# Placing the halves of every weight tile 64 and 192 bytes, modulo 256, from the rows that stream through TensorE

## The chip, the cores and the metric

The kernel runs on one core of a Trainium2 chip. The metric is the device time of one execution in microseconds (us), lower is better; the times given are medians over executions.

## The reference

A trunk of four decoder layers works on `x` of 256 tokens by 1024 features in float32. Each layer is a feed-forward block (SwiGLU, hidden size 2816), a token mixer (latent attention, differential attention, a Mamba-2 scan, then latent attention again) and a second feed-forward block. Each of the twelve sub-layers is

```
y = fn(x * (1 + scale) + shift)
x = layernorm(alpha * x + weight * gate * y)
```

where shift, scale and gate come from `silu(c) @ w_mod + b_mod`. Almost all of the arithmetic lies in the products of 256 token rows with weight matrices:

```
gate, up = split(h @ w_in, 2)          # 1024 x 5632
y = (silu(gate) * up) @ w_out          # 2816 x 1024
```

About 500 MB of float32 weights are read once, and every product has to keep float32 accuracy.

## The kernel before, in words

**Three products for one.** TensorE multiplies in the type `F32R`, which holds fewer bits than float32. So each operand is split into a high half (the value as the type holds it) and a low half (what is missing), and `mm3` (line 485) issues three matmuls for each product: high weights with high rows, high weights with low rows, low weights with high rows.

```
T.matmul(out=ps, lhsT=wh, rhs=xh, start=first, stop=False)
T.matmul(out=ps, lhsT=wh, rhs=xl, start=False, stop=False)
T.matmul(out=ps, lhsT=wl, rhs=xh, start=False, stop=last)
```

The weights (`lhsT`, 128 columns, 512 bytes of each SBUF partition) are loaded into the array, and the activations (`rhs`, 256 columns, 1024 bytes of each partition) stream through. The weights of a matmul are loaded again for each of the three, and the load of the next matmul's weights lies beside the streaming of the present one.

**Where the operands lie.** All of SBUF is laid out once, by the calls of `pool` in `trunk` (lines 442 to 453). The rows that stream are in `hwh` and `hwl` (high and low halves of the modulated input) or in tiles of `g` (hidden activations). Every tile between `g` and the weight ring has a size that is a multiple of 256 bytes (`g` 2048, `wraw` 4096, `hwh` and `hwl` 9216, and so on), so all rows that stream in the full products start at the same address modulo 256. The split weights are in the ring `wr` of 16 tiles of 4096 bytes, and behind the ring come the small tiles: constants, masks, statistics. With `WSTEP = 16`, `Slots.__init__` (line 117) puts an unused gap of 16 floats (64 bytes) behind every second tile of the ring. So tiles `wr0` and `wr1` lie 0 bytes, modulo 256, from the rows, `wr2` and `wr3` 64, `wr4` and `wr5` 128, `wr6` and `wr7` 192, `wr8` and `wr9` 0 again, and so on: both halves of a weight have one offset, and the four offsets take turns.

**How the ring is filled.** `take` (line 593) fetches the next weights in half items of four 128-row blocks by 256 columns: SP issues one DMA of 512 KB into `wraw`, ScalarE copies it into the tile of the high half, and VectorE subtracts and writes the low half (`split`, line 507). One half item serves 4 x 2 x 3 = 24 matmuls. Ring tiles are handed out by `Program.place` (line 207) in the order in which they came free; after some sub-layers the pairs come out with the high half in the odd tile.

**What sets the order.** A planner in the program (`Program.schedule`) orders all instructions from fixed costs that know nothing of addresses; each engine then runs its list in order, and semaphores hold it where data are late. Between the half items, `gm_mac` streams the modulation weights `w_mod` through `wraw` and accumulates them on VectorE, by the quotas in `PLAN`.

At the start of each sub-layer `pre_mms` (line 874) multiplies the rows before their normalization is known. There the rows are 258 columns wide, and `hwh` steps by 288 floats (1152 bytes) from one block of 128 to the next, so odd blocks lie 128 bytes off.

Of the kernel before, what the change touches and what calls it, by code (L numbers as in the profile page):

```python
# [10 lines left out]
F32 = mybir.dt.float32  # L11
F32R = mybir.dt.float32r
# [43 lines left out]
class Ref:  # L56


    def __init__(self, root, fns):
        self.root, self.fns, self.ap = root, fns, None  # L60
# [52 lines left out]
class Slots:  # L113

    def __init__(self, pool, name, n, elems, psum=False, dt=F32, fresh=False, step=0):
        self.pool, self.name, self.elems, self.psum, self.dt, self.fresh = pool, name, elems, psum, dt, fresh
        self.tiles = []
        for i in range(n):  # L120
            self.tiles.append(self.make(i, dt))
            if step and i % 2:
                pool.tile([128, step], F32, name=f"{name}gap{i}", tag=f"{name}gap{i}")
        self.free = list(range(n))
        self.hist, self.old, self.owner = [[] for _ in range(n)], [[] for _ in range(n)], [None] * n

# [292 lines left out]

WHOLE = (4, 7, 10)  # L420

WSTEP = 16

DEFER = {0: 3, 1: 3}

# [2 lines left out]
def trunk(ctx: ExitStack, tc: tile.TileContext, consts, x, c, positions, w_mod, b_mod, ln_g, ln_b,  # L428
# [8 lines left out]
    sb = ctx.enter_context(tc.tile_pool(name="sb", bufs=1))  # L437
    pp = ctx.enter_context(tc.tile_pool(name="pp", bufs=1, space=PSUM))
    PW, HP = S + 2, 288
    slots = {}  # L440

    def pool(name, n, elems, dt=F32, step=0):
        slots[name] = Slots(sb, name, n, elems, dt=dt, fresh=name == "g", step=step)

    slots["mm"] = slots["aux"] = Slots(pp, "mm", 8, 512, True)
    for name, n, elems in (("g", 25, 512), ("wraw", 8, 1024), ("gacc", 1, 3072), ("res", 1, 2048),
                           ("t256", 14, 256), ("sd", 1, 512), ("re", 1, 512)):
        pool(name, n, elems)
    for name, n, elems in (("hwh", 1, KD * HP), ("hwl", 1, KD * HP)):
        pool(name, n, elems, F32R)  # L450
    pool("wr", 16, 1024, F32R, WSTEP)
    for name, n, elems in (("dtr", 1, 128), ("w0", 1, 32), ("modc", 6, 24)):
        pool(name, n, elems)

# [308 lines left out]
    class Tail:  # L763
        def __init__(self, s, res, weight):
            self.s, self.d = s, res
            self.weight, self.w = weight, None
# [878 lines left out]
```

## Time and profile before

| what | value |
|---|---|
| median of three executions | 2103.96 us (2102.66 to 2103.96) |
| the profiled execution's own time | 2103.96 us |
| its span in the profile | 2102.2 us |
| granted TensorE clock, mean over the span | 0.998 |
| PE (matmuls) busy | 2074.9 us, 99% |
| DVE (VectorE), ACT (ScalarE) busy | 1713.0 us (81%), 1190.2 us (57%) |
| HBM traffic | 500.73 MB read, 239 GB/s over the span |

The profile names engines PE (matmuls of TensorE), PEld (its weight loads), DVE, ACT, POOL and SP. PE's busy time comes from matmuls whose ends are modelled, and consecutive matmuls overlap: one lasts some 280 ns, but the next starts after some 117 ns. So the pace of PE is read from starts and counts, not from the duration of one. A granted clock of 1.00 is 2.4 GHz.

### The profile page before, as it was taken

How to read it: one execution, taken by the hardware profiler on the slowest of the kernel's cores; microseconds unless marked ns; L12 is line 12 of the kernel's file. 1: busy time of each engine (PE TensorE's matmuls, PEld its weight loads, DVE VectorE, ACT ScalarE, POOL GpSimd, SP SyncE). 2: the span in 40 equal slices, each digit the busy share in tenths (PEclk: the TensorE clock that was granted, in tenths of full speed). 3: DMA queues.
4: the chain of work that ended last, by engine and by line, in shares of the span. 5: the costliest groups of instructions: out<-in, count | busy, mean ns of one | idle time of the engine just before them, and what ended most of it. 6: DMA issues, size and time to landing. Idle time of an engine off the chain costs nothing. (4 is left out here: it accounts for less than half of the span.)

```text
span 2102.2 us, 42927 instructions
## 1 busy us (share of the span) xinstructions
PE 2074.9 (99%) x17287; PEld 2011.6 (96%) x17287; DVE 1713.0 (81%) x2745; ACT 1190.2 (57%) x1836; POOL 98.5 (5%) x112
## 2 busy tenths in 40 slices
PE   8999999999999999999999999999999999999998
PEld 6999999999999999999999988899999999999998
DVE  4888899887887879977988798879887988879744
ACT  3554687536544786644654475547545644577543
POOL 0000100000000101000000011000000000100000
PEclk9999999999999999999999999999999999999999
DMA  9899657995989435997698654356986889545861
GB/s 312 281 346 326 206 188 249 342 304 187 319 309 324 149 103 161 350 326 256 191 354 304 206 159 140 112 157 197 355 281 205 302 305 323 163 130 186 261 186 45
DMA packets 410227, 504.58 MB, mean 240 GB/s; under 512 B 21937, under 2 KB 371244, under 8 KB 410028
## 3 DMA queue, kind: packets, MB, share of 16 engines
q1 hardware_dynamic: 410028, 501.84, 72.5%
q8 instruction: 135, 2.21, 0.4%
q14 instruction: 64, 0.52, 0.1%
HBM read 500.73 MB, written 1.05 MB: 239 GB/s over the span
## 5 line engine op out<-in xcount | busy, mean ns | idle before, releaser
L400 PE MATMUL mm<-hwh,wr 128*128 128x256 f32 (+1 forms) x6736 | 1222.2, 283 | 3.7 <-ACT hwh L400 1.9
L400 PEld LDWEIGHTS mm<-hwh,wr 128*128 128x128 f32 x6736 | 1041.1, 189 | 19.9 <-issue 14.1
L400 ACT ACTIVATE wr<-wraw 128x1024 fp32r<-128x1024 f32 (+3 forms) x705 | 700.7, 1003 | 577.2 <-PE mm L400 242.9
L400 PE MATMUL mm<-hwl,wr 128*128 128x256 f32 (+1 forms) x3368 | 955.7, 284 | 4.9 <-DVE hwl L400 4.8
L400 DVE TENSOR_TENSOR wr<-wraw,wr 128x1024 fp32r<-128x1024 f32 (+3 forms) x691 | 793.7, 1165 | 172.4 <-ACT wr L400 169.1
L400 PE MATMUL mm<-g,wr 128*128 128x256 f32 x5496 | 665.2, 282 | 1.4 <-DVE g L400 0.9
L400 PEld LDWEIGHTS mm<-g,wr 128*128 128x128 f32 x5496 | 652.9, 189 | 12.3 <-issue 8.3
L400 PEld LDWEIGHTS mm<-hwl,wr 128*128 128x128 f32 x3368 | 637.4, 189 | 11.1 <-DVE hwl L400 6.8
L400 DVE SCALAR_TENSOR_TENSOR gacc<-wraw,condc,gacc 128x1024 f32<-128x1024 f32 x238 | 307.2, 1291 | 7.9 <-DMA wraw<-in_w_mod_dram 7.2
L400 ACT ACTIVATE g<-mm 128x512 f32<-128x512 f32 (+4 forms) x208 | 105.7, 521 | 100.3 <-PE mm L400 98.7
L400 ACT ACTIVATE g<-g 128x512 fp32r<-128x512 f32 (+1 forms) x104 | 63.3, 625 | 36.0 <-DVE g L400 35.6
L400 PE MATMUL mm<-g,g 128*128 128x128 f32 (+2 forms) x464 | 81.6, 312 | 0.0
L400 DVE TENSOR_TENSOR g<-g,g 128x512 fp32r<-128x512 f32 (+2 forms) x111 | 75.4, 699 | 4.2 <-ACT g L400 3.4
L400 DVE TENSOR_TENSOR res<-res,re 128x256 f32<-128x256 f32 x171 | 68.0, 418 | 8.2 <-ACT re L400 7.9
L400 DVE TENSOR_TENSOR g<-g,mm 128x512 f32<-128x512 f32 x81 | 54.9, 680 | 19.6 <-PE mm L400 16.9
L400 PEld LDWEIGHTS mm<-g,g 128*128 128x128 f32 (+1 forms) x464 | 57.9, 175 | 7.4 <-ACT g L400 0.5
L400 ACT ACTIVATE t<-res 128x256 f32<-128x256 f32 x84 | 34.8, 416 | 48.1 <-DVE res L400 47.9
L400 POOL TENSOR_TENSOR res<-res,t 128x256 f32<-128x256 f32 x28 | 25.4, 932 | 708.9 <-ACT t L400 624.9
L400 DVE TENSOR_TENSOR res<-res,t 128x256 f32<-128x256 f32 x56 | 31.7, 581 | 23.9 <-ACT t L400 23.9
L400 DVE SCALAR_TENSOR_TENSOR res<-mm,gw,res 128x256 f32<-128x256 f32 x84 | 39.2, 475 | 14.2 <-PE mm L400 14.2
L400 ACT ACTIVATE t<-res,abcol 128x256 f32<-128x256 f32 x72 | 43.2, 601 | 9.3 <-DVE res L400 8.0
L400 ACT ACTIVATE res<-res,abcol 128x256 f32<-128x256 f32 x88 | 48.0, 588 | 0.0
(198 smaller groups left out, 1158.5 us busy)
## 6 DMA issues: line engine op xcount, KB each, us to landing
wraw<-in_ffn_w_in_dram SPq DMA_DIRECT2D x340, 512.0 KB, 6.1
wraw<-in_w_mod_dram SPq DMA_DIRECT2D x272, 512.0 KB, 6.8
wraw<-in_ffn_w_out_dram SPq DMA_DIRECT2D x128, 512.0 KB, 5.7
wraw<-in_ffn_w_out_dram SPq DMA_DIRECT2D x64, 384.0 KB, 5.7
wraw<-in_ssm_w_in_dram SPq DMA_DIRECT2D x32, 512.0 KB, 4.3
wraw<-in_diff_w_in_dram SPq DMA_DIRECT2D x24, 512.0 KB, 4.3
wraw<-in_w_mod_dram SPq DMA_DIRECT2D x32, 256.0 KB, 6.2
wraw<-in_mla_w_out_dram SPq DMA_DIRECT2D x16, 512.0 KB, 4.6
```

Of the source, the lines that this page charges most:

```text
L400: getattr(eng.real, method)(*[real(a) for a in args], **{k: real(v) for k, v in one.items()})
```

## The change

`Slots.__init__` takes a list of gaps in place of a step, and puts gap number i ahead of tile number i. For `wr` the list is 16 floats and then 15 times 32 floats, that is 64 bytes ahead of `wr0` and 128 bytes ahead of every later tile.

```diff
-    def __init__(self, pool, name, n, elems, psum=False, dt=F32, fresh=False, step=0):
+    def __init__(self, pool, name, n, elems, psum=False, dt=F32, fresh=False, gaps=()):
...
         for i in range(n):
+            if gaps and gaps[i]:
+                pool.tile([128, gaps[i]], F32, name=f"{name}gap{i}", tag=f"{name}gap{i}")
             self.tiles.append(self.make(i, dt))
-            if step and i % 2:
-                pool.tile([128, step], F32, name=f"{name}gap{i}", tag=f"{name}gap{i}")
...
-WSTEP = 16
+WGAPS = [16] + [32] * 15
...
-    pool("wr", 16, 1024, F32R, WSTEP)
+    pool("wr", 16, 1024, F32R, WGAPS)
```

All even tiles of the ring now lie 64 bytes, modulo 256, from the rows that stream, and all odd tiles 192. The ring takes 1472 bytes more of each partition, and the small tiles behind it move by that. Which tile a half item gets, and the order of instructions on every engine, stay as they were; the names in the built order differ in their running number alone.

This is a place in the engine order of PE where two half items are worked off in turns of six matmuls (start of a feed-forward block); a name such as `wr7_132` is ring tile 7 with the running number of its allocation. Before:

```order
L400 MATMUL mm1_62<-hwh0_120,wr7_132 128x256
L400 MATMUL mm1_62<-hwl0_121,wr7_132 128x256
L400 MATMUL mm1_62<-hwh0_120,wr6_131 128x256
L400 MATMUL mm1_62<-hwh0_120,wr7_132 128x256
L400 MATMUL mm1_62<-hwl0_121,wr7_132 128x256
L400 MATMUL mm1_62<-hwh0_120,wr6_131 128x256
L400 MATMUL mm7_68<-hwh0_120,wr11_138 128x256
L400 MATMUL mm7_68<-hwl0_121,wr11_138 128x256
L400 MATMUL mm7_68<-hwh0_120,wr10_137 128x256
```

And now:

```order
L400 MATMUL mm1_62<-hwh0_120,wr7_137 128x256
L400 MATMUL mm1_62<-hwl0_121,wr7_137 128x256
L400 MATMUL mm1_62<-hwh0_120,wr6_135 128x256
L400 MATMUL mm1_62<-hwh0_120,wr7_137 128x256
L400 MATMUL mm1_62<-hwl0_121,wr7_137 128x256
L400 MATMUL mm1_62<-hwh0_120,wr6_135 128x256
L400 MATMUL mm7_68<-hwh0_120,wr11_145 128x256
L400 MATMUL mm7_68<-hwl0_121,wr11_145 128x256
L400 MATMUL mm7_68<-hwh0_120,wr10_143 128x256
```

Nothing moved. The tile that is used twice holds the high half; here that is the odd one. Before, `wr7` and `wr6` lay at 192 and `wr11` and `wr10` at 64, so the offset changed every six matmuls; now the odd tiles lie at 192 and the even ones at 64, so it changes twice in every three.

The second place is a run of half items later on PE, before; the first row of each is shown:

```order
L400 MATMUL mm6_67<-hwh0_120,wr0_122 128x256
...
L400 MATMUL mm1_62<-hwh0_120,wr12_140 128x256
...
L400 MATMUL mm1_62<-hwh0_120,wr14_143 128x256
...
L400 MATMUL mm7_68<-hwh0_120,wr2_125 128x256
...
L400 MATMUL mm7_68<-hwh0_120,wr9_135 128x256
...
L400 MATMUL mm2_63<-hwh0_120,wr5_129 128x256
...
L400 MATMUL mm2_63<-hwh0_120,wr11_138 128x256
...
L400 MATMUL mm3_64<-hwh0_120,wr7_132 128x256
```

By the layout before, these eight half items lie at offsets 0, 128, 192, 64, 0, 128, 64 and 192. After the change each of them has one half at 64 and one at 192.

## Rows read from the trace of the kernel before

**Rows 1.** The page: span, busy time of the engines, and the granted clock in 40 slices.

```profile
span 2102.2 us, 42927 instructions
...
PE 2074.9 (99%) x17287; PEld 2011.6 (96%) x17287; DVE 1713.0 (81%) x2745; ACT 1190.2 (57%) x1836; POOL 98.5 (5%) x112
...
PEclk9999999999999999999999999999999999999999
```

**Rows 2.** Waits of PE, the longest kind: us in total, times, longest.

```profile
PE mm L400 <- DVE hwl L400: 4.8, 7, 1.6
```

**Rows 3.** Groups of PE by form: count, busy us, mean ns, idle before.

```profile
L400 PE MATMUL mm<-hwh,wr 128*128 128x256 f32 x5984 | 1082.5, 283 | 3.7 <-ACT hwh L400 1.9 <-ACT g L400 1.0 <-DVE wr L400 0.5
L400 PE MATMUL mm<-hwl,wr 128*128 128x256 f32 x2992 | 847.3, 283 | 1.8 <-DVE hwl L400 1.8
L400 PE MATMUL mm<-g,wr 128*128 128x256 f32 x5496 | 665.2, 282 | 1.4 <-DVE g L400 0.9 <-ACT g L400 0.2
L400 PE MATMUL mm<-hwh,wr 128*128 128x258 f32 x752 | 141.0, 285 | 0.0
L400 PE MATMUL mm<-hwl,wr 128*128 128x258 f32 x376 | 108.4, 288 | 3.1 <-DVE hwl L400 3.1
```

**Rows 4.** Windows, PE instructions on ring tiles alone: busy us (count), PEclk, DMA, GB/s.

```profile
360.00:480.00 120.00, 118.58 (x1012) 1.00 0.94 322
840.00:960.00 120.00, 119.50 (x1009) 1.00 0.92 317
1040.00:1160.00 120.00, 118.64 (x1022) 1.00 0.96 332
1640.00:1760.00 120.00, 118.64 (x1006) 1.00 0.93 321
```

**Rows 5.** Timeline of PE, second run of half items: start us, us, instruction.

```profile
1459.21 0.40 PE L400 MATMUL mm<-hwh,wr 128*128 128x256 f32 x2
...
1462.08 0.40 PE L400 MATMUL mm<-hwh,wr 128*128 128x256 f32 x2
...
1464.92 0.40 PE L400 MATMUL mm<-hwh,wr 128*128 128x256 f32 x2
...
1467.75 0.39 PE L400 MATMUL mm<-hwh,wr 128*128 128x256 f32 x2
...
1470.47 0.40 PE L400 MATMUL mm<-hwh,wr 128*128 128x256 f32 x2
...
1473.35 0.40 PE L400 MATMUL mm<-hwh,wr 128*128 128x256 f32 x2
...
1476.19 0.40 PE L400 MATMUL mm<-hwh,wr 128*128 128x256 f32 x2
...
1479.02 0.40 PE L400 MATMUL mm<-hwh,wr 128*128 128x256 f32 x2
...
1481.85 0.40 PE L400 MATMUL mm<-hwh,wr 128*128 128x256 f32 x2
```

**Rows 6.** Timeline of PE, the place with turns of six matmuls.

```profile
1029.32 0.40 PE L400 MATMUL mm<-hwh,wr 128*128 128x256 f32 x2
...
1034.77 0.39 PE L400 MATMUL mm<-hwh,wr 128*128 128x256 f32 x2
```

**Rows 7.** Timeline of PE in a stretch with 258 columns.

```profile
1017.85 0.41 PE L400 MATMUL mm<-hwh,wr 128*128 128x258 f32 x2
...
1023.60 0.40 PE L400 MATMUL mm<-hwh,wr 128*128 128x258 f32 x2
```

**Rows 8.** Windows, all: PE, PEld, DVE, ACT, POOL busy us (count), PEclk, DMA, GB/s.

```profile
280.00:320.00 40.00, 38.33 (x301) 35.98 (x301) 38.93 (x80) 33.51 (x71) 2.34 (x3) 1.00 0.63 198
360.00:400.00 40.00, 40.00 (x345) 40.00 (x344) 38.35 (x41) 26.05 (x32) 1.33 (x1) 1.00 1.04 366
1240.00:1280.00 40.00, 39.41 (x305) 33.78 (x306) 38.23 (x58) 26.09 (x42) 6.49 (x2) 1.00 0.60 175
```

More of the change, by code (lines that the diff above doesn't have):

```diff
@@ L440, in trunk, with pool @@
     slots = {}
-    def pool(name, n, elems, dt=F32, step=0):
-        slots[name] = Slots(sb, name, n, elems, dt=dt, fresh=name == "g", step=step)
+    def pool(name, n, elems, dt=F32, gaps=()):
+        slots[name] = Slots(sb, name, n, elems, dt=dt, fresh=name == "g", gaps=gaps)
     slots["mm"] = slots["aux"] = Slots(pp, "mm", 8, 512, True)
```

## The prediction, made before the change was run

> **What bounds the kernel now.** I read the page's busy times first: PE is busy for 2074.9 of 2102.2 us and runs at full clock in every slice, the other engines are at 81% or less [rows 1]. The waits of PE come next, because a busy PE could still be waiting in small pieces: the longest kind, for the low halves of the rows, is 4.8 us in seven pieces [rows 2]. So the time is the number of matmuls times their pace, and the pace is what to look at. The groups of PE by form give the number: 5984 + 2992 + 5496 = 14,472 matmuls of 256 columns with weights from the ring, and 752 + 376 = 1128 of 258 columns [rows 3]; all others are 17,287 - 15,600 = 1687.
>
> The mean in those rows (283 ns) is the length of one matmul and not its share of the time, since they overlap. The pace comes from windows inside feed-forward blocks, counting ring matmuls alone: 475.36 us for 1012 + 1009 + 1022 + 1006 = 4049, that is **117.4 ns** each [rows 4]. At 2.4 GHz, 256 columns are 106.7 ns, so each matmul takes some 10 ns more than its streaming.
>
> The timeline shows that these 10 ns are not the same everywhere. It gives the start of a matmul to 10 ns, which is enough over the 24 of a half item. In the second run of half items [rows 5], differences of successive starts divided by 24 are:
>
> - offset 0 (`wr0`, `wr9`): 2.87 and 2.88 us, 119.6 to 120 ns
> - offset 128 (`wr12`, `wr5`): 2.84 and 2.84 us, 118.3 ns
> - offset 192 after 128 (`wr14`): 2.83 us, 117.9 ns
> - offset 64 right after that 192 (`wr2`): 2.72 us, **113.3 ns**
> - offset 64 after 128 (`wr11`): 2.83 us, 117.9 ns
> - offset 192 right after that 64 (`wr7`): 2.83 us, 117.9 ns
>
> The instructions, shapes and clock are the same; what differs is where the weights lie relative to the rows. Offsets 0 and 128 are never quick here. Offsets 64 and 192 have two paces, a quick one (113.3) and a slow one (117.9), and it seems to be the history that decides: the change from 192 to 64 turned slow into quick, the change from 64 to 192 left slow as it was. I take it for a collision of the two reads of PE, the weights being loaded and the rows that stream, with a phase that locks. That is a reading, not a row.
>
> The third piece of evidence is the place where offsets 192 and 64 change places every six matmuls: 48 matmuls from 1029.32 to 1034.77 us, 113.5 ns each [rows 6]. Seven changes in either direction, and the quick pace holds through all of them.
>
> **The change, part by part.** *Instructions.* None is added, removed or moved on any engine, no DMA changes its size or its queue.
>
> *The 14,472 matmuls of 256 columns.* After the change every load comes from offset 64 or 192, and each three contain one change from 192 to 64 and one back. The quick pace survives both changes [rows 6], and a slow one meets, every three matmuls, the change that lifted it in [rows 5]. So I take the quick pace throughout: 117.4 - 113.4 = 4.0 ns for each, 14,472 x 4.0 = **57.9 us**. The end most in favour would be the streaming time of 106.7 ns; no row comes below 113.3, so I don't take it as a bound. The other end is the slow pace of 117.9 ns, 0.5 ns worse than now: +7 us.
>
> *Rule against it.* A 24-matmul half item takes 2.72 us at one place and 2.88 us at another [rows 5]. The Trainium skill, page "SBUF — State Buffer", section "Who interferes with whom", gives PE two independent read ports, one for the streaming operand and one for weights, and says "PE and ACT never wait on anyone"; by that the offset is worth nothing and the time stays. The trace disagrees, with the 0.16 us between these two half items beside it; the page's case is the second rival.
>
> *The 1128 matmuls of 258 columns.* Their pace is (1023.60 - 1017.85) / 48 = 119.8 ns [rows 7], over all offsets. The start of each stream there also shifts by 128 bytes from block to block, and no stretch of them is quick. I take no gain; the bounds are 0 and 119.8 - 113.4 = 6.4 ns each, 7 us.
>
> *The other 1687 matmuls.* Constants behind the ring move by 1472 bytes, so transposes and sums read other offsets. No row prices this. Most of them are short or stand among waits; by the widest spread of [rows 5] over a third of them, 560 x 6.7 ns, it is under 4 us either way. I take 0.
>
> *Writers.* ScalarE and VectorE write the same tiles at new offsets. They run beside PE with 19 to 43% of idle time [rows 1], so a few ns for each are hidden; if that cover were gone, VectorE would be the engine to bound, which comes next.
>
> *What is late next.* PE asks for half items 3.5% faster. DMA gives 317 to 332 GB/s in the busy blocks [rows 4] and would have to give 328 to 344; it gave 366 in one stretch [rows 8], so it follows. VectorE is the tighter one: 38.93, 38.35 and 38.23 of 40 us in three windows [rows 8]. In the first and third PE already loses time (38.33 and 39.41 busy), so nothing is gained there. There are some such stretches at every entry of a sub-layer; I take 1000 matmuls without gain, 1000 x 4.0 = 4 us lost.
>
> Sum: -57.9 + 4 = **-54 us**. The profiled execution took 2103.96 us itself, equal to the median of the runs (its span is 2102.2), so no correction: 2104 - 54 = **2050 us**.
>
> **The rivals.**
>
> *The two paces stay mixed.* If the phase locks anew at each break (evacuation, transpose, wait), 64 and 192 give what they give now on average. Four offsets in equal shares make 117.4, and 0 and 128 have 119.7 and 118.3; so 64 and 192 together average (4 x 117.4 - 119.7 - 118.3) / 2 = 115.8 ns, halfway between their paces. Gain: 1.6 x 14,472 = 23 us, time **2081**. For it: at 1476 us both offsets stay slow for 48 matmuls [rows 5]. Against it: that run has no change from 192 to 64, and now there is one in every three.
>
> *The offset does nothing.* The differences of [rows 5] come from something else that takes turns with the ring, such as what VectorE or the DMA touch at that moment: **2104**. The page named above would give this. Against it: equal offsets repeat to 0.01 us a half item apart in time, which a coincidence with other engines would not.
>
> *The slow pace locks (the other side).* Each three now holds 64, 64 and 192 (or 192, 192 and 64) in close turns, which no place before has; the shortest turn is six. If a single matmul at 192 is too short for the phase to shift, the change back to 64 lifts nothing, every matmul takes the 117.9 ns of 1476 to 1482 us, and the change from 64 to 192 may add to it. Price: 0.5 ns x 14,472 = +7 us, **2111**; if the first matmul after each change cost as much as offset 0, (2 x 117.9 + 119.7) / 3 = 118.5 ns, +16 us. It decides if fewer than about one in ten of the threes run quick: (117.9 - 117.4) / (117.9 - 113.4) = 0.11. Against it: the quick pace was lost at no change in [rows 6], and one quick three should be enough to keep it.
>
> *VectorE takes the bound* not only at entries. The middle window of [rows 8] would go from 38.35 to 38.35 x 1.035 = 39.7 of 40 us, which is full for all practical purposes. If a quarter of the span were so, a quarter of the gain would go, 57.9 / 4 = 14.5 us in place of 4: 2060. It lies inside the forecast's range.
>
> **How the numbers follow.** Quick pace, with VectorE binding more or less: 0.70, from 2039 (57.9 + 7 of the 258 columns) to 2062. Mixed paces: 0.16, from 2062 to 2092. No effect: 0.07. Slow lock: 0.07. Predicted is the likeliest, **2050 us**. The range from **2039 to 2084** takes in the forecast's own and the better half of the mixed case, some eight tenths. A change of 0.2% (4.2 us) is about what a measurement of this kernel can tell from none. Faster by more: 0.70 + 0.16 = **0.86**; within 0.2%: **0.07**; slower by more: **0.07**.
>
> **What would show it.** Right: in the timeline, half items start every 2.72 us wherever they lie in the ring, [rows 4] become some 1040 to 1055 matmuls per 120 us, PE's waits stay under some 30 us in total, and the groups of [rows 3] have the same counts. The 258-column stretches stay near 119.8 ns. Mixed paces would show as half items of 2.72 and of 2.83 us side by side; a slow lock as 2.83 or 2.85 us everywhere. VectorE as the bound would show as waits of PE on `wr` from DVE. The prediction is wrong if the pace depends on the offsets' closeness in time and not on each load alone, for then nothing in the trace of before shows the new pattern.

## The result, and the profile after

| | before | after |
|---|---|---|
| median | 2103.96 us | **2055.41 us** (2054.43 to 2057.71, 4 runs) |
| ratio, 95% interval | 1 | 0.9773 (0.9754 to 0.9792) |
| profiled execution, its span | 2103.96, 2102.2 us | 2055.8, 2054.0 us |
| PE busy, and the rest of the span | 2074.9 + 27.3 us | 2024.8 + 29.2 us |

A fourth execution of the kernel before took 5206.11 us and is not counted.

The change is worth 48.5 us of the 54 forecast; the predicted time was 2050. The first thing to read is how the fall of the span, 48.2 us, divides: PE's busy time fell by 50.1 us, and the time in which it was idle grew by 1.9. The page after, to be held against [rows 1]:

```profile
span 2054.0 us, 42927 instructions
...
PE 2024.8 (99%) x17287; PEld 1961.4 (95%) x17287; DVE 1714.5 (83%) x2745; ACT 1193.6 (58%) x1836; POOL 98.0 (5%) x112
...
PEclk9999999999999999999999999999999999999999
```

The counts and the clock are those of before, and DVE and ACT were busy for about the same time. So PE did the same work faster. The groups by form say which work (columns as in [rows 3]):

```profile
L400 PE MATMUL mm<-hwh,wr 128*128 128x256 f32 x5984 | 1050.9, 279 | 4.2 <-ACT hwh L400 1.9 <-DVE wr L400 1.0 <-ACT g L400 0.9
L400 PE MATMUL mm<-hwl,wr 128*128 128x256 f32 x2992 | 837.2, 280 | 1.9 <-DVE hwl L400 1.9
L400 PE MATMUL mm<-g,wr 128*128 128x256 f32 x5496 | 646.2, 278 | 1.5 <-DVE g L400 0.9 <-ACT g L400 0.3
L400 PE MATMUL mm<-hwh,wr 128*128 128x258 f32 x752 | 140.8, 285 | 0.0
```

The three groups of 256 columns each lost some 3 to 4 ns in the mean of one (283, 283 and 282 before); the group of 258 columns did not (285 in both). The windows of [rows 4] give the pace, ring tiles alone:

```profile
360.00:480.00 120.00, 118.58 (x1040) 1.00 0.98 333
840.00:960.00 120.00, 118.58 (x1044) 1.00 0.97 333
1040.00:1160.00 120.00, 118.64 (x1041) 1.00 0.95 323
1640.00:1760.00 120.00, 118.64 (x1042) 1.00 0.93 311
```

They hold 4167 matmuls in 474.44 us, **113.86 ns** each, against 117.40 before. The same can be seen start by start. The half items of [rows 5], from the timeline after:

```profile
1429.99 0.39 PE L400 MATMUL mm<-hwh,wr 128*128 128x256 f32 x2
...
1432.71 0.39 PE L400 MATMUL mm<-hwh,wr 128*128 128x256 f32 x2
...
1435.43 0.39 PE L400 MATMUL mm<-hwh,wr 128*128 128x256 f32 x2
...
1451.75 0.39 PE L400 MATMUL mm<-hwh,wr 128*128 128x256 f32 x2
...
```

Each of the eight takes 2.72 us, 113.3 ns for each matmul; before, one of the eight did. But look at the second place, the one with turns of six [rows 6]:

```profile
1006.12 0.40 PE L400 MATMUL mm<-hwh,wr 128*128 128x256 f32 x2
...
1011.83 0.40 PE L400 MATMUL mm<-hwh,wr 128*128 128x256 f32 x2
...
1012.54 0.40 PE L400 MATMUL mm<-hwh,wr 128*128 128x256 f32 x2
...
1017.98 0.39 PE L400 MATMUL mm<-hwh,wr 128*128 128x256 f32 x2
```

The same 48 matmuls that took 5.45 us before, and on which the prediction built, take 5.71 us now, 119.0 ns each. Here the change made the ring slower. The slow stretch begins with the first matmul of 256 columns at 1000.53 us, and from 1012.54 on it is over: the next 48 matmuls take 5.44 us, 113.3 ns. By the order of instructions, every pair from 1000.53 us on has its high half in an odd tile, at 192; the first with the high half at 64 starts with the second matmul of the row of 1011.83.

That is a pattern. I took the differences of successive starts (those under 140 ns, with a ring matmul on either side) and averaged them by where the high half lies. After the change, pairs with the high half at 64 take 113.64 ns (8235 matmuls), pairs with the high half at 192 take 114.35 (5772), all together 113.93. In the slow stretches five starts of some 118 ns and one of some 124 take turns, 119.0 ns on the mean; one of 94 matmuls begins at 297.57 us, the one above has some 100.

The same trace shows what the order does to the pace. Take the uninterrupted stretches in which at least 24 starts keep one order, and compare the first twelve starts with the last twelve (slow is a mean over 115.5 ns). With the high half at 64, 22 stretches began slow and all of them ended quick, and 71 were quick throughout. With the high half at 192, 15 began slow and all of them ended slow, and 64 were quick throughout.

### The profile page after: what moved, and what is told of

The parts are those of the page before. It is cut to its first block, busy times and chain, and to the rows that moved or that the text cites. A ratio compares the mean times of both kernels' runs of the same rounds, so it can differ in the third digit from the quotient of the medians.

```text
span 2054.0 us, 42927 instructions
## 1 busy us (share of the span) xinstructions
PE 2024.8 (99%) x17287; PEld 1961.4 (95%) x17287; DVE 1714.5 (83%) x2745; ACT 1193.6 (58%) x1836; POOL 98.0 (5%) x112
## 5 line engine op out<-in xcount | busy, mean ns | idle before, releaser
L400 PE MATMUL mm<-hwh,wr 128*128 128x256 f32 (+1 forms) x6736 | 1190.4, 280 | 4.2 <-ACT hwh L400 1.9
L400 PEld LDWEIGHTS mm<-hwh,wr 128*128 128x128 f32 x6736 | 1028.4, 188 | 20.4 <-issue 14.0
L400 PE MATMUL mm<-hwl,wr 128*128 128x256 f32 (+1 forms) x3368 | 945.8, 281 | 5.8 <-DVE hwl L400 5.8
L400 PE MATMUL mm<-g,wr 128*128 128x256 f32 x5496 | 646.2, 278 | 1.5 <-DVE g L400 0.9
L400 PEld LDWEIGHTS mm<-g,wr 128*128 128x128 f32 x5496 | 634.2, 188 | 12.4 <-issue 7.4
```

What stands on the lines that cost most here:

```text
L400: getattr(eng.real, method)(*[real(a) for a in args], **{k: real(v) for k, v in one.items()})
```

## The experiments

All of them are built on the changed kernel. The ring `wr` of 16 tiles becomes two rings of 8, `wrh` for high halves and `wrl` for low halves, so that a half can never land on the other's offset. The order of PE's instructions stays the same. The first edit in full:

```diff
-            wh, wl = buf("wr", [128, b - a, ncols], F32R), buf("wr", [128, b - a, ncols], F32R)
+            wh, wl = buf("wrh", [128, b - a, ncols], F32R), buf("wrl", [128, b - a, ncols], F32R)
...
-    pool("wr", 16, 1024, F32R, WGAPS)
+    pool("wrh", 8, 1024, F32R, [16] + [0] * 7)
+    pool("wrl", 8, 1024, F32R, [32] + [0] * 7)
```

Every later one changes the numbers in brackets (gaps in floats, of 4 bytes), or changes or adds one more line.

**High at 64, low at 192, never swapped.**

> Two rings in place of one: every high half at 64, every low half at 192, never swapped. Same order of instructions. Theory (which half lies where decides whether a slow pace is lifted; with the high half at 64 it is): the stretches of 118 to 124 ns that are left in the changed kernel go, 256-column matmuls come to 113.4 to 113.6 ns from 113.9, some 5 to 7 us less than the changed kernel: 2048 to 2051. Rival (the pace is drawn at each break, whichever half lies where): as the changed kernel, 2054 to 2058.

2052.05 us (2050.86 to 2055.16, 5 runs), ratio 0.9744 (0.9731 to 0.9758). By time alone that lies between the two expectations, in runs whose median of before was 2106.05 and not 2103.96. The trace decides: its span is 2049.1 us, 4.9 less than after, and the place of turns of six reads

```profile
1003.01 0.28 PE L400 MATMUL mm<-hwh,wrl 128*128 128x256 f32 x1
...
1008.45 0.28 PE L400 MATMUL mm<-hwh,wrl 128*128 128x256 f32 x1
```

which is 5.44 us again. The mean of all starts is 113.59 ns, 0.34 less than after; over 14,007 matmuls that is 4.8 us, the whole difference of the spans. Slow entries still occur, but none lasts: from the first slow start (117 ns or more) to the last there are never more than 11 matmuls.

**The opposite order: high at 192, low at 64.**

```diff
-    pool("wrh", 8, 1024, F32R, [16] + [0] * 7)
+    pool("wrh", 8, 1024, F32R, [48] + [0] * 7)
```

> The same two rings, swapped: every high half at 192, every low half at 64. Theory: what enters slow stays slow until the next break, cycles of 118, 118, 124 ns; about half of all runs of matmuls enter slow, so 2070 to 2110, and never below the changed kernel. Rival (drawn at each break): 2054 to 2058. Rival of the forecast (a collision that depends on the set of offsets alone): equal to the run with the halves the other way round.

2075.67 us, span 2073.9, one run. The timeline has both paces, each over 192 matmuls:

```profile
610.10 0.28 PE L400 MATMUL mm<-hwh,wrl 128*128 128x256 f32 x1
...
632.93 0.28 PE L400 MATMUL mm<-g,wrl 128*128 128x256 f32 x1
...
1445.09 0.28 PE L400 MATMUL mm<-hwh,wrl 128*128 128x256 f32 x1
...
1466.85 0.28 PE L400 MATMUL mm<-hwh,wrl 128*128 128x256 f32 x1
```

22.83 us are 118.9 ns, 21.76 are 113.3. The slow stretch at 609 us lasts for all 555 matmuls of its block; its cycle is not the expected 118, 118, 124 but five starts near 118 and one near 124. The pair of offsets is that of the first experiment, and each three still contains one change from 192 to 64 and one back; only which of the two comes twice is different, and the lift is gone.

**Both halves at one offset: 64, 0 and 192.** These take the change of offset inside the three away.

```diff
-    pool("wrl", 8, 1024, F32R, [32] + [0] * 7)
+    pool("wrl", 8, 1024, F32R, [0] + [0] * 7)
```

with 16, 0 and 48 floats ahead of `wrh`.

> Both halves at 64, so that no offset changes within a product. Theory (both paces lock at 64, and only a change of offset lifts the slow one): each run keeps the pace that it enters with, 113.3 or 117.9 ns; 2060 to 2105, half items of 2.72 and of 2.83 us side by side, none in between. Rival (64 is simply a good offset): 2050 to 2056.

> Both halves at 0. Theory (the offset of the weights from the rows that stream sets the pace): 120 ns everywhere, 14,051 steady matmuls x (120 - 117.5) = +34 us on the kernel before, 2130 to 2140. Rival (what ran beside the matmuls made the difference, and it took turns with the ring): 2095 to 2110.

> Both halves 192 bytes from the rows, the two rings otherwise as in e1. Theory (two paces that each run of matmuls keeps from its entry; only the change from 192 to 64 lifts the slow one): there is no change at all, so whole runs lie at 113.3 ns or at 117.8 ns side by side, with more slow ones than at 64 alone, since in the kernel before 192 was the slower of the two offsets (2297 of 3518 matmuls slow, against 1563 of 3430 at 64); 2072 to 2105 us. Rival (192 by itself is a good offset, and 64 was the one that lost): 2050 to 2060 us.

Measured, one execution each: 2071.51 us with both at 64, 2137.39 with both at 0, 2095.27 with both at 192. All three lie where the theory put them, and outside what the rivals expected. With both at 64, the kernel has the two paces again, here at the place of [rows 6] (48 matmuls) and in the half items of [rows 5] (192):

```profile
1012.92 0.28 PE L400 MATMUL mm<-hwh,wrl 128*128 128x256 f32 x1
...
1018.36 0.28 PE L400 MATMUL mm<-hwh,wrl 128*128 128x256 f32 x1
...
1439.60 0.28 PE L400 MATMUL mm<-hwh,wrl 128*128 128x256 f32 x1
...
1462.21 0.28 PE L400 MATMUL mm<-hwh,wrl 128*128 128x256 f32 x1
```

5.44 us are 113.3 ns, 22.61 are 117.8. With both at 0 there is one pace; the half items of [rows 5] take 23.04 us, 120.0 ns each:

```profile
1482.81 0.28 PE L400 MATMUL mm<-hwh,wrl 128*128 128x256 f32 x1
...
1505.85 0.28 PE L400 MATMUL mm<-hwh,wrl 128*128 128x256 f32 x1
```

The share of matmuls at 116 ns or less is 65% at 64, 20% at 192 and under 1% at 0. So 64 and 192 are not equal either: what they have in common is the pair of paces, and 64 enters the quick one more often.

**The rows of 258 columns.** One more edit on the first experiment takes away the shift by 128 bytes from block to block.

```diff
-    PW, HP = S + 2, 288
+    PW, HP = S + 2, 320
```

> e1 with one more edit: blocks of the 258 columns step by 320 floats (1280 bytes, a multiple of 256) instead of 288, so that there too each high half lies at 64 and each low half at 192 from the rows, where now every second block has them at 192 and 64. Theory A (the shift by 128 bytes from block to block keeps these stretches slow): the 1128 matmuls go from about 120.5 ns toward 113.4 to 114.4, 6 to 7 us less than e1, some 2044 to 2047 us. Theory B (a row of 258 columns, 1032 bytes, never is quick, whatever the offset): as e1, 2050 to 2055 us, 120 ns in these stretches.

2053.33 us (2052.46 to 2053.79, 4 runs), ratio 0.9745 (0.973 to 0.976): theory B. The place of [rows 7] takes 5.80 us for 48, 120.8 ns:

```profile
994.01 0.28 PE L400 MATMUL mm<-hwh,wrl 128*128 128x258 f32 x1
...
999.81 0.28 PE L400 MATMUL mm<-hwh,wrl 128*128 128x258 f32 x1
```

The shift was not what kept these stretches slow. That 258 columns are 1032 bytes, and so no multiple of 256, remains as a possible reason, but it is not shown: a stretch of this kind with 256 columns wasn't tried.

**The changed kernel and the first experiment again, on one chip.**

> The changed kernel as it is, beside the other two on one chip. Theory (where the ring hands out pairs with the high half at 192, slow runs do not lift, which costs about 0.35 ns on the mean of 14,051 matmuls): 4 to 6 us over e1_again. Rival (the difference of e1 to the changed kernel was one of chips or runs): within 2 us of e1_again.

> High halves always at 64, low halves always at 192, the same kernel as e1, beside the changed kernel on one chip. Theory: 4 to 6 us under after_again. Rival: within 2 us of it.

2057.21 us (2054.43 to 2061.0, 5 runs), ratio 0.9763 (0.9746 to 0.978), and 2053.76 (2052.95 to 2054.91, 4 runs), ratio 0.9748 (0.9733 to 0.9763). The 3.5 us between the medians lie between the two expectations and the intervals of the ratios overlap, so by times alone the two are not told apart. The spans of these two traces (2059.2 and 2051.2 us) don't serve either, because the granted clock differs. It fell to 0.5, its lower level of 1.2 GHz, for 6.8 us near 314 us in the changed kernel and for 3.4 us near 311 in the first experiment, shortly after PE had waited 2 us for `hwl`; in the first pair of traces, with a like wait, it stayed at 1.00. These are the windows (columns as in [rows 8]): the changed kernel in the second trace and in the first, then the first experiment in the second trace and in the first.

```profile
314.20:321.00 6.80, 6.80 (x34) 6.80 (x33) 5.32 (x14) 1.49 (x4) 0.95 (x1) 0.50 0.37 116
...
315.00:321.00 6.00, 6.00 (x52) 6.00 (x52) 4.97 (x13) 3.46 (x5) 0.96 (x1) 1.00 0.75 212
...
311.00:314.40 3.40, 3.40 (x19) 3.40 (x17) 2.63 (x6) 2.33 (x6) 0.00 (x0) 0.50 0.02 5
...
311.00:315.00 4.00, 4.00 (x36) 4.00 (x35) 3.97 (x10) 1.46 (x4) 0.42 (x1) 1.00 0.23 58
```

The means of the starts under 140 ns leave such stretches out, and they tell the two kernels apart as in the first pair: 113.94 and 113.57 ns, with 114.36 for pairs whose high half lies at 192.

**Is it the distance from the rows, or the address itself?** An unused tile ahead of everything moves rows and weights alike.

```diff
+    sb.tile([128, 16], F32, name="pad", tag="pad")
     slots["mm"] = slots["aux"] = Slots(pp, "mm", 8, 512, True)
```

> e1 with an unused tile of 16 floats ahead of everything in SBUF, so that rows and weights all move by 64 bytes and their distance stays: high halves at 64, low halves at 192 from the rows. Theory (the distance of weights and rows decides): as e1, 2049 to 2056 us and 113.3 to 114 ns. Rival (the weights' own address modulo 256 decides, or the rows' own): another mix of paces, 2065 us or more.

2050.66 us (2050.18 to 2057.18, 4 runs), ratio 0.9748 (0.9728 to 0.9769), span 2049.0, mean of the starts 113.58 ns. The 192 matmuls of [rows 5] take 21.76 us, 113.3 ns each:

```profile
1425.62 0.28 PE L400 MATMUL mm<-hwh,wrl 128*128 128x256 f32 x1
...
1447.38 0.28 PE L400 MATMUL mm<-hwh,wrl 128*128 128x256 f32 x1
```

The distance decides, as far as one shift by 64 bytes can show it.

**How exact must it be?** 32 bytes less, 32 bytes more, and the low half alone moved to 128 (8, 24 and 16 floats ahead of `wrh`; 32, 32 and 16 ahead of `wrl`).

> e1 with both distances 32 bytes smaller: high halves at 32, low halves at 160. Theory A (what counts is that the distance is no multiple of 128 bytes and that it changes by 128 from high to low): about as e1, 2048 to 2060 us. Theory B (64 and 192 are the only good places, the further from a multiple of 128 the better): between e1 and both at 0, 2065 to 2125 us. Below 2048 us would mean a quicker pace than any seen, under 113.3 ns.

> e1 with both distances 32 bytes larger: high halves at 96, low halves at 224. Theory A of e8: about as e1, 2048 to 2060 us. Theory B of e8: 2065 to 2125 us. If e8 and this differ from each other, the sign of the shift counts too, and the best place is not symmetric about 64 and 192.

> e1 with the low halves at 128 instead of 192. Theory (what lifts a slow run is the change from 192 to 64; 128 is never quick by itself): two of three matmuls can be at 113.3 ns, the third at 118 to 120; with no lift, or the lift undone at each low half, 2070 to 2105 us. Rival (any change of distance from low to high half lifts): 2050 to 2065 us.

High at 32 and low at 160: 2116.46 us (2114.38 to 2123.23, 5 runs), ratio 1.0056 (1.0037 to 1.0075). High at 96 and low at 224: 2109.73 us (2106.77 to 2112.69, 10 runs), ratio 1.0019 (1.001 to 1.0029). High at 64 and low at 128: 2117.06 us, one run. All three are no better than the kernel before. For the first two theory A fell and theory B held; their ratios also differ from each other, beyond the intervals, so the sign of the shift counts. The third lost more than the theory had allowed. In that third kernel the 192 matmuls of [rows 5] take 22.70 us, 118.2 ns each:

```profile
1470.52 0.28 PE L400 MATMUL mm<-hwh,wrl 128*128 128x256 f32 x1
...
1493.22 0.28 PE L400 MATMUL mm<-hwh,wrl 128*128 128x256 f32 x1
```

In the third, two of three matmuls still load from 64, and none settles at 113.3 ns: from one start to the next they go 116, 119, 120, 118, 116, 118, 114, 124, 120 ns. So one load in three at 128 is enough to keep all three from the quick pace; how it does so is not shown.

## Why the prediction was right, point by point

**What bounds the kernel**: right. No wait, DMA or other engine set the end, the pace of one kind of matmul did, and it has moved the time by itself from 2050.66 us to 2137.39 with the same instructions in the same order on PE. One reading under it was too coarse: a 9 in the row of the clock says 90% or more of a slice, and in the trace of before the clock was at 0.5 for 3.4 us at 1213.8 us. The trace of after has the like at 1187.4 us, so the comparison isn't touched.

**The 14,472 matmuls of 256 columns**: the mechanism held in the main, one step of it failed, and the term was too large. It was put at 4.0 ns each, from 117.4 to 113.4, 57.9 us. The windows show 3.54 ns, to 113.86, and PE's busy time fell by 50.1 us. The step that failed is "a slow one meets, every three matmuls, the change that lifted it". The change from 192 to 64 does not lift a slow stretch by itself. With the high half at 192, each three has that change too, and 555 matmuls in a row stayed slow (second experiment). What lifts, within 11 matmuls in the first experiment, is the order 64, 64, 192. In the changed kernel 5772 of 14,007 steady matmuls came in the other order; with the order held to 64, 64, 192 the mean is 113.59 ns and the span 2049.1 us, 53.1 under that of before, where the forecast's sum was 54. The other half of the argument held: the quick pace survives the changes in either order, for 192 matmuls at 1445 us of the second experiment.

The lift in [rows 5] was itself no accident, but it was a lift from one half item to the next. In the trace of before, counting places where at least 18 starts at one offset meet at least 18 at another without a break, and judging each by the mean of its last twelve, a slow pace turned quick in 12 of 13 changes from 192 to 64, in none of 18 from 64 to 192, and in all 27 from 0 to 192. So the change from 192 to 64 lifted where 64 was then kept, it is not the only change that lifts, and nothing there said what a single load at 64 between loads at 192 would do.

The prediction had named this as its sign of being wrong: that the pace depends on the offsets' closeness in time and not on each load alone. That is what the second experiment and the one with the low half at 128 show. That the point forecast came as near as it did is partly luck: the ring handed out 8235 of the 14,007 matmuls in the order that lifts, and most stretches in the other order entered at the quick pace, neither of which the prediction had worked out.

**The 258 columns**: right, at no gain (119.8 ns before). The place of [rows 7] takes 5.79 us for 48 after the change, 120.6 ns:

```profile
994.62 0.40 PE L400 MATMUL mm<-hwh,wr 128*128 128x258 f32 x2
...
1000.41 0.40 PE L400 MATMUL mm<-hwh,wr 128*128 128x258 f32 x2
```

The reason that the prediction set beside it, the shift of the rows, was wrong.

**The entries, 4 us lost**: right in kind. The 301 matmuls of the first window of [rows 8] take as long after the change as before, 40.17 and 40.08 us from the first start to the last:

```profile
273.61:313.73 40.12, 38.37 (x301) 36.03 (x301) 38.95 (x80) 33.53 (x71) 2.32 (x3) 1.00 0.64 198
```

They take 39.98 us with the order held, and 39.90 with everything at 0, where the ring matmuls are slowest. With both halves at 64 and with the pair swapped they take 41.66 and 41.85, but there the granted clock fell to 0.5 for 3.4 and 6.8 us near 315 us, which it did not in the four others. The pace of PE does not set this stretch. VectorE is busy for 38.95 us of it, which fits the prediction; that VectorE is the cause was not tried. Elsewhere the loss was small. PE's waits after, the longest kind and the one on the ring:

```profile
PE mm L400 <- DVE hwl L400: 5.8, 9, 1.7
PE mm L400 <- DMA wraw<-in_w_mod_dram: 3.5, 1, 3.5
...
PE mm L400 <- DVE wr L400: 1.0, 1, 1.0
```

The longest kind was 4.8 us before [rows 2], so it grew by 1.0. The gain of 50.1 us less 1.9 us of idle is the result.

**The rivals.** *Mixed paces* did not decide the changed kernel, but they are what the other three arrangements of 64 and 192 give: 2071.51, 2075.67 and 2095.27 us, around the 2081 worked out for it. *The offset does nothing* is excluded: 2137.39 and 2052.05 us differ by two unused gaps. For this kind of matmul that also speaks against what the Trainium skill, page "SBUF — State Buffer", section "Who interferes with whom", says of PE, that its two read ports are independent and that it never waits on anyone, as far as the prediction took it to mean that the offset is worth nothing: a start every 120.0 ns with both halves at 0, every 113.3 ns at 64 and 192. The runs do not show in which port or part the time is lost, so the collision of two reads that the prediction took for the cause stays a reading. *The slow pace locks* came true where the pair is swapped and the stretch enters slow, 15 of the 79 such stretches counted above, the place of turns of six among them; its pace there is 119.0 ns, not the 117.9 or 118.5 that the rival had. Had the ring handed out every pair swapped, the time would have been about that of the second experiment, 2075.67 us, still under 2104, because many stretches enter at the quick pace. *VectorE takes the bound* beyond the entries did not occur: it was busy for 83% of the span after, and its waits are those above.

## What to carry to other kernels

In this kernel, where the weights are loaded anew for every matmul, the distance modulo 256 bytes between the weights and the rows that stream is a parameter like a tile size: 4% of the time lay between the worst and the best choice, at the same instructions. Where a kernel of this kind is built, it is worth trying, and it should be set for each operand by its role, in separate rings, and not left to the order in which buffers come free. Such a pace is found by counting starts in a window with no waits, since the busy share (99% in every version here) says nothing of it.

## What the runs showed that was not expected

- Two paces for one instruction, each kept for hundreds of matmuls with nothing but the entry to tell them apart: 113.3 and 117.8 ns with both halves at 64 (2071.51 us in all). The prediction had the two paces, but expected every change from 192 to 64 to lift the slow one.
- The order of 64 and 192 within a three matters, though both orders have the same two changes: 64, 64, 192 lifts a slow stretch within 11 matmuls, 192, 192, 64 keeps one at 118.9 ns over 555. Why is open.
- The good places are narrow: 32 bytes to either side cost 59 and 66 us (2109.73 and 2116.46 us, against 2050.66 on the same chip for 64 and 192 with everything moved by 64 bytes). Whether smaller steps do too was not tried.
- The fastest versions keep the order with two rings: 2052.05, 2053.76 and, with everything moved by 64 bytes, 2050.66 us, against 2055.41 and 2057.21 for the changed kernel.
